# Moving two token halves against each other in a planned kernel: new distances at the stage boundaries, new head timing, new priorities

## The chip, the cores and the metric

The kernel runs on one core of a Trainium2 chip. A core has TensorE (PE, matrix products), VectorE (DVE), ScalarE (ACT), GpSimd (POOL) and SyncE (SP, which issues the DMAs); each works through its own list of instructions in order and waits at semaphores for the others. The metric is the device time of one launch in microseconds (us). Before the change it is 2561.59 us, the median of three runs (2561.55 to 2563.88).

## The reference

One step of an encoder with two layers and 1024 features, over 512 prompt tokens and 32 sample tokens. Each layer is a gated feed-forward part (FFN) of half weight, a token mixer, and a second FFN; before and after each part stands an RMS norm, and shift, scale and gate of it ("modulation") come from a conditioning vector through a matrix of 9 x 1024 columns per layer. The mixer of layer 0 is retention with 8 heads, that of layer 1 differential attention with 8 heads against keys and values made once after layer 0.

```python
for l in range(DEPTH):
    mod = (jax.nn.silu(c) @ w_ada[l] + b_ada[l]).reshape(b, N_MOD, D_MODEL)
    h = modulate(x, g_norm[l, 0], mod[:, 0], mod[:, 1])
    x = x + HALF * mod[:, 2, None] * rms_norm(swiglu(h, w_ffn_in[l, 0], w_ffn_out[l, 0]), g_norm[l, 1])
    h = modulate(x, g_norm[l, 2], mod[:, 3], mod[:, 4])
    # y: retention (l = 0) or differential attention (l = 1)
    x = x + mod[:, 5, None] * rms_norm(y, g_norm[l, 3])
    h = modulate(x, g_norm[l, 4], mod[:, 6], mod[:, 7])
    x = x + HALF * mod[:, 8, None] * rms_norm(swiglu(h, w_ffn_in[l, 1], w_ffn_out[l, 1]), g_norm[l, 5])
    if l == N_A - 1:
        k, v = shared_kv(x, c, pos, w_ada_kv, b_ada_kv, g_kv, w_kv)
```

## The kernel before

The features lie on the partitions and the 544 tokens on the free axis, cut into half A (tokens 0 to 255) and half B (the other 256 prompt tokens and the 32 sample tokens, 288 columns). Every product with a weight is cut into **units**: one block of 128 output features for one half. A unit is 6 or 8 k-steps of three matmuls (the operands are split into a high and a low part), all on line 599, 128x256 for A and 128x288 for B. There are 368 units for each half, in the order of the stages: FFN (1) of layer 0, retention, FFN (2) of layer 0, the shared keys and values, FFN (1) of layer 1, the eight query units (Q), the eight units of the attention's output product (OB), FFN (2) of layer 1.

A weight block is loaded by DMA, cast on ACT to its high part (line 578) and subtracted on DVE for its low part (line 581). Four such blocks (`w`) are held at once. If A and B use a block within a short stretch of the order, one load serves both; otherwise it is loaded and converted twice.

Between two stages each half goes through a **chain**: the last output product is added up (L918), squares are taken and summed on DVE (L824, L828), PE sums over the partitions (L711), POOL takes the root (L717), PE spreads the result (L722), DVE scales and adds into the residual stream X (L877, L880); then the same norm again for the next stage (L828, L711, L717, L722), and DVE and ACT make its eight operands (L749, L758, L764). The units of the next stage wait for these. While half A is in its chain, units of half B keep PE busy, and the other way round. `_path()` writes down, as pairs of unit numbers (a, b), how far A may be when B is at a given place. For a boundary e with entry (x, hold, y, z) of the table `BND`, A reaches e while B is x units short of it, B then goes on by `hold` units alone, and A goes y units past e before B enters; z sets over how many units the two come together before and after. The list `ATT` gives the pairs for layer 1 one by one. `plan()` turns the pairs into one list of (unit, half), interleaved evenly between two pairs.

The instruction lists of the engines are written by a list scheduler inside the kernel (`Sched`): each piece of work has a priority (smaller first), units have 1000 and their place in the list, work in the chains about 1 to 2. It takes five PSUM banks for units and three for all else; a unit's bank is free when its product has been read out, which for an FFN's output product is the addition on L918. The modulation is made in ten blocks of four PE steps (8 matmuls of 128x512 each, L504), each of which needs two loads of 1 MB; a step has the priority `ADA_HI` once its block is due, and a block comes due when the order reaches a unit number shifted by `ADA_LEAD`. `CONV_P` is the priority of the casts on ACT, `ROPE_LEAD` says how many units ahead the rotary tables are fetched, `RETH` how many retention heads may hold memory at once.

Of the kernel before, what the change touches and what calls it, by code (L numbers as in the profile page):

```python
# [49 lines left out]
def _path():  # L50
# [3 lines left out]
    for e in ((0, 1), (0, 2), "kv", (1, 0)):  # L54
        x, hold, y, z = BND.get(e, BND0)
        p += [((e, -z), (e, -z - L0)), ((e, 0), (e, -x)), ((e, 0), (e, -x + hold)), ((e, y), (e, 0)),
              ((e, y + z), (e, y + z - L0))]
    return p + [((e0, a), (e1, b)) for e0, a, e1, b in ATT]


BND0 = (7, 7, 7, 14)
BND = {(0, 1): (7, 7, 6, 10), (0, 2): (7, 7, 6, 5), 'kv': (8, 8, 6, 8), (1, 0): (0, 1, 4, 6)}
Q, OB, F2 = (1, 1), "ob", (1, 2)
ATT = [(Q, -67, Q, -75), (Q, 4, Q, -34), (Q, 8, Q, -23), (OB, 0, Q, -31), (OB, -8, Q, -13), (F2, 1, Q, -16),
       (F2, -6, Q, 0), (F2, 6, Q, -2), (F2, 37, OB, -1), (F2, 55, OB, 1), (F2, 55, F2, 0), (F2, 70, F2, -4)]
NSLOT = (34, 34)
NW = 4
NRAW = 3
# [52 lines left out]
class Sched:  # L121
# [14 lines left out]
    def go(self, gen, prio):  # L136
        self.live += 1
        self._at(self.now, [gen, prio, None], None)
# [184 lines left out]
def yoco_step(ctx: ExitStack, tc: tile.TileContext, I, O):  # L323
# [39 lines left out]
    def fa(r, n=None, o=0, p0=0, p1=P):  # L363
        n = r[1] - o if n is None else n
        return FA[p0:p1, r[0] + o:r[0] + o + n]
# [15 lines left out]
    def pe(cost, fn, pr=None):  # L381
        return ("PE", cost, fn) if pr is None else ("PE", cost, fn, pr)
# [109 lines left out]
    def ada():  # L492
        yield ready["sc"]
        yield from ada_first()
        for u in range(1, 10):
            b = yield from bank(miscb, -1)
            for k0 in range(0, 8, ADA_K):
# [3 lines left out]
                def mm(u=u, k0=k0, b=b):  # L501
                    for k in range(k0, k0 + ADA_K):
                        for g in range(4):
                            te.matmul(PS[b][32 * g:32 * g + 32, :], lhsT=SC[:, k, :],  # L504
                                      rhs=fa(ada_buf[u, k], 512, g * 512), start=(k == 0), stop=(k == 7))
                yield pe(TILED + ADA_K * 900, mm, ADA_HI if u <= due[0] else ADA_LO)
                for k in range(k0, k0 + ADA_K):
# [48 lines left out]
    def w_dma():  # L556
        for d in loads:
            u = d.unit
            r = (yield ("get", rawbuf, 1))[0]
            d.raw = (r[0], u.nk * P)  # L560

            def one(d=d, u=u, r=r):
                yield dma(u.nk * P * P * 4, fa(d.raw).rearrange("p (k f) -> p k f", f=P), u.wap, W_P.get(u.idx, 10))
                d.rawbuf = r
                S.set(d.raw_ev)
            go(one(), 0)

    def w_conv():
        for d in loads:
            w = (yield ("get", wpool, 1))[0]  # L570
            d.w = w
            yield d.raw_ev
            nk = d.unit.nk
            n = nk * P
            hi = WT[w][:, 0, :nk, :].rearrange("p k f -> p (k f)")
            lo = WT[w][:, 1, :nk, :].rearrange("p k f -> p (k f)")
            src = fa(d.raw)
            yield act(n, lambda: nc.scalar.copy(hi, src))  # L578

# [36 lines left out]
    def gate_at(n):  # L616
        ev = Ev()
        gates.append((n, ev))
        return ev
# [356 lines left out]
    def ret_prep(gate):  # L976
        yield gate
        r = yield from get(2 * NTOK, 1)
        ret["rope"] = r
        yield dma(P * 2 * NTOK * 4, fa(r), I["rope_a"], 15)  # L980
        S.set(ret["rope_ev"])
# [58 lines left out]
    def retention(hops, yevs):  # L1040
        w = I["w_in_a"][0]
        ret["rope_ev"] = Ev()
        ret["sem"] = Pool(range(RETH))
        go(ret_prep(gate_at(len(units) - ROPE_LEAD)), 15)
        st = Stage(hops)
# [276 lines left out]
    def kv_prep(gate):  # L1322
        yield gate
        r = yield from get(2 * NTOK, 1)
        kv["rope"] = r
        yield dma(P * 2 * NTOK * 4, fa(r), I["rope_b"], 15)
        S.set(kv["rope_ev"])
# [25 lines left out]
    def shared_kv(hops):  # L1353
        w = I["w_kv"]
        go(kv_prep(gate_at(len(units) - ROPE_LEAD)), 15)
        st = Stage(hops)
# [429 lines left out]
    for l in range(2):  # L1786
        m0 = 11 * l
        for s in range(3):
            if l or s:
                mark((l, s))  # L1790

            ada_due.append((max(0, len(units) + ADA_LEAD), 6 if l == 0 and s == 2 else (m0 + 3 * s + 4) // 2))
            if s != 1:
# [22 lines left out]
    go(w_dma(), 10)  # L1816
    go(w_conv(), CONV_P)
    plan()
# [7 lines left out]

TILED = 190
ADA_K = 2
ROPE_LEAD = 30
ADA_X = 4  # L1830
CT_P = -0.5
XB_P = 1.5
# [1 line left out]

TANH = (1,)
FIN_P = 0
CONV_P = 0
NEXT_P = 25
ADA_HI = 900
ADA_LO = 5000  # L1840
ADA_FIRST = 0
ADA_LEAD = -52
ARENA_N = 20600

YW = 2
RETH = 4
ATH = 3
BSEM = 3

# [112 lines left out]
```

## Time and profile before

| | |
|---|---|
| Median of three runs | 2561.59 us |
| Time of the profiled execution | 2562.68 us |
| Its span, first to last instruction | 2560.9 us |
| Mean granted TensorE clock | 0.993 |
| PE busy | 2496.2 us (97%) |
| DVE busy | 1400.1 us (55%) |
| ACT busy | 1091.3 us (43%) |
| Weight conversions on DVE (L581) | 552 |

The page names the time in which an engine worked; PE's span less its busy time is 64.7 us. The chain of work that ended last lies to 86% on PE. A share over the whole span says little here: DVE is busy for 10.87 of 50 us in one stretch and 49.58 of 50 in another, so what an idle gap of PE is worth has to be read where it stands.

### The profile page before, as it was taken

How to read it: one execution, taken by the hardware profiler on the slowest of the kernel's cores; microseconds unless marked ns; L12 is line 12 of the kernel's file. 1: busy time of each engine (PE TensorE's matmuls, PEld its weight loads, DVE VectorE, ACT ScalarE, POOL GpSimd, SP SyncE). 2: the span in 40 equal slices, each digit the busy share in tenths (PEclk: the TensorE clock that was granted, in tenths of full speed). 3: DMA queues.
4: the chain of work that ended last, by engine and by line, in shares of the span. 5: the costliest groups of instructions: out<-in, count | busy, mean ns of one | idle time of the engine just before them, and what ended most of it. 6: DMA issues, size and time to landing. Idle time of an engine off the chain costs nothing.

```text
span 2560.9 us, 48166 instructions
## 1 busy us (share of the span) xinstructions
PE 2496.2 (97%) x19848; PEld 2379.2 (93%) x19848; DVE 1400.1 (55%) x2604; ACT 1091.3 (43%) x2159; POOL 58.5 (2%) x88
## 2 busy tenths in 40 slices
PE   7999999999999999999999999999899999999998
PEld 5889999899999997999998899999699988898998
DVE  5223334955424457323338944555786987768555
ACT  4222224643333355322126533444565655465434
POOL 0000000000000000000000000000000000000000
PEclk9999999999999999999999999999899999999999
DMA  8662323642222237522226853555655445545553
GB/s 321 263 239 84 98 90 107 227 152 95 80 80 91 76 109 279 189 88 95 91 76 221 271 173 127 167 180 190 241 194 175 159 160 185 178 161 169 165 165 109
DMA packets 122235, 404.61 MB, mean 158 GB/s; under 512 B 15008, under 2 KB 33568, under 8 KB 111776
## 3 DMA queue, kind: packets, MB, share of 16 engines
q1 hardware_dynamic: 122016, 401.54, 45.9%
q8 instruction: 155, 2.54, 0.4%
q14 instruction: 64, 0.52, 0.1%
HBM read 388.25 MB, written 13.24 MB: 157 GB/s over the span
## 4 chain that ended last, share of the span: by engine, by line
PE 86%; DVE 8%; ACT 3%; issue 2%; DMA 1%; POOL 0%; SPq 0%; POOLq 0%; DVEq 0%; ACTq 0%
PE ps L599 77%; DVE w L581 2%; PE ps L504 2%; ACT w L578 1%; DVE FA L1025 1%; DVE FA L749 1%; DVE r L764 1%; PE ps L1601 1%; PE ps L1231 1%; PE ps L1219 1%; ACT FA L858 0%; PE ps L1540 0%; DMA X<-in_xb 0%; PE ps L1594 0%; DVE FA L828 0%
## 5 line engine op out<-in xcount | busy, mean ns | idle before, releaser
L599 PE MATMUL ps<-r,w 128*128 128x256 f32 (+1 forms) x17280 | 2269.4, 291 | 15.8 <-ACT r L758 11.5
L599 PEld LDWEIGHTS ps<-r,w 128*128 128x128 f32 x17280 | 2205.5, 191 | 55.7 <-issue 25.9
L581 DVE TENSOR_TENSOR w<-FA,w 128x1024 fp32r<-128x1024 f32 (+1 forms) x552 | 658.9, 1194 | 572.4 <-ACT w L578 567.5
L578 ACT CAST w<-FA 128x1024 fp32r<-128x1024 f32 (+1 forms) x552 | 564.6, 1023 | 883.5 <-PE ps L599 799.8
L965 DVE TENSOR_TENSOR FA<-ps,FA 128x256 f32<-128x256 f32 (+1 forms) x88 | 38.8, 441 | 192.5 <-PE ps L599 191.9
L929 ACT CAST r<-FA 128x288 fp32r<-128x288 f32 (+1 forms) x176 | 73.1, 416 | 107.3 <-DVE FA L965 88.3
L918 DVE TENSOR_TENSOR FA<-ps,FA 128x288 f32<-128x288 f32 (+1 forms) x144 | 62.3, 438 | 97.7 <-PE ps L599 96.2
L930 DVE TENSOR_TENSOR r<-FA,r 128x288 fp32r<-128x288 f32 (+1 forms) x176 | 76.6, 437 | 21.9 <-ACT r L929 21.5
L758 ACT ACTIVATE r<-FA,MOD 128x256 fp32r<-128x256 f32 (+1 forms) x168 | 63.1, 437 | 51.7 <-DVE FA L749 51.3
L828 DVE TENSOR_TENSOR FA<-FA 128x256 f32<-128x256 f32 (+1 forms) x168 | 73.1, 436 | 12.7 <-ACT FA L824 11.1
L504 PE MATMUL ps<-FA,SC 128*32 128x512 f32 x576 | 70.7, 605 | 5.6 <-DMA FA<-in_ada 5.6
L962 DVE SCALAR_TENSOR_TENSOR FA<-ps,FA 128x288 f32<-128x288 f32 (+1 forms) x88 | 38.4, 439 | 49.9 <-PE ps L599 49.8
L953 ACT ACTIVATE FA<-ps 128x256 f32<-128x256 f32 (+1 forms) x88 | 34.5, 393 | 69.7 <-PE ps L599 69.6
L749 DVE SCALAR_TENSOR_TENSOR FA<-X,DRV,ps 128x256 f32<-128x256 f32 (+1 forms) x168 | 57.3, 396 | 9.5 <-PE ps L722 9.3
L717 POOL TENSOR_TENSOR FA<-FA,NHALF 128x2 f32<-128x2 f32 (+1 forms) x24 | 21.7, 906 | 1774.8 <-DVE FA L715 1687.0
L858 ACT ACTIVATE FA<-FA,DRV 128x256 f32<-128x256 f32 (+1 forms) x144 | 59.1, 442 | 2.9
L764 DVE SCALAR_TENSOR_TENSOR r<-FA,MOD,r 128x256 fp32r<-128x256 f32 (+1 forms) x168 | 58.5, 400 | 0.4 <-ACT r L758 0.2
L1025 DVE TENSOR_TENSOR FA<-ps,FA 64x288 f32<-64x288 f32 (+1 forms) x128 | 56.1, 438 | 2.0
L916 ACT COPY FA<-ps 128x288 f32<-128x288 f32 (+1 forms) x96 | 36.3, 380 | 44.6 <-PE ps L599 44.6
L1021 DVE TENSOR_TENSOR FA<-ps,FA 128x256 f32<-128x256 f32 (+1 forms) x64 | 27.8, 437 | 48.9 <-PE ps L599 48.8
L504 PEld LDWEIGHTS ps<-FA,SC 128*32 128x32 f32 x576 | 14.8, 109 | 33.6 <-issue 22.4
L824 ACT ACTIVATE FA<-FA 128x256 f32<-128x256 f32 (+1 forms) x84 | 35.7, 425 | 15.5 <-DVE FA L918 14.9
(149 smaller groups left out, 1120.6 us busy)
## 6 DMA issues: line engine op xcount, KB each, us to landing
FA<-in_w_ffn_in SPq DMA_DIRECT2D x261, 512.0 KB, 3.3
FA<-in_ada SPq DMA_DIRECT2D x80, 1024.0 KB, 7.1
FA<-in_w_ffn_out SPq DMA_DIRECT2D x95, 512.0 KB, 3.5
FA<-in_w_in_a SPq DMA_DIRECT2D x58, 512.0 KB, 3.2
FA<-in_w_ffn_out SPq DMA_DIRECT2D x62, 384.0 KB, 3.1
FA<-in_w_kv SPq DMA_DIRECT2D x24, 512.0 KB, 4.4
FA<-in_w_out_a SPq DMA_DIRECT2D x20, 512.0 KB, 3.6
FA<-in_w_q_b SPq DMA_DIRECT2D x16, 512.0 KB, 3.4
```

The source lines that it names most:

```text
L504: te.matmul(PS[b][32 * g:32 * g + 32, :], lhsT=SC[:, k, :], rhs=fa(ada_buf[u, k], 512, g * 512), start=(k == 0), stop=(k == 7))
L578: yield act(n, lambda: nc.scalar.copy(hi, src))
L581: yield dve(n, lambda: nc.vector.tensor_tensor(lo, src, hi.bitcast(F32), ALU.subtract))
L599: te.matmul(PS[b][:, :n], lhsT=w[:, a, k, :], rhs=x, start=(k == 0 and j == 0), stop=(k == u.nk - 1 and j == 2))
L749: nc.vector.scalar_tensor_tensor(fa(z, c1 - c0, o), X[:, f, c0:c1], DRV[:, gi, f, s:s + 1], PS[Rb][:, o:o + c1 - c0], ALU.mult, ALU.mult)
L758: nc.scalar.activation(op.hi(H, c0, c1), fa(z, c1 - c0, o), AF.Identity, bias=MOD[:, mi, f, s:s + 1])
L764: nc.vector.scalar_tensor_tensor(op.lo(H, c0, c1), fa(z, c1 - c0, o), MOD[:, mi, f, s:s + 1], op.hi(H, c0, c1).bitcast(F32), ALU.add, ALU. ...
L828: yield dve(n, lambda: nc.vector.tensor_tensor(acc, acc, fa(t), ALU.add))
L918: yield dvp(n, lambda: nc.vector.tensor_tensor(Y[:, f, c], PS[b][:, :n], Y[:, f, c], ALU.add), 15)
L929: yield act(n, lambda: nc.scalar.copy(op.hi(H), src), pr)
L930: yield dve(n, lambda: nc.vector.tensor_tensor(op.lo(H), src, op.hi(H).bitcast(F32), ALU.subtract), pr)
L1025: nc.vector.tensor_tensor(fa(t1, n, n, x, x + 64), PS[b][y:y + 64, :n], fa(rr, n, NTOK + c.start, y, y + 64), ALU.mult)
```

## The change

Only tables and constants change; what is computed, the units and the matmuls stay as they are.

- `BND`: A goes further past three of the boundaries before B enters (y from 6 to 7, 6 to 10 and 6 to 10), and B goes on by one unit more during A's chain at two of them (hold 9 with x 8).
- `ATT`: when A reaches the queries, B is 40 units short of them and not some 36; in both versions it is 23 short when A's eight query units are through, so that now two units of B stand beside each of A's. Before the last FFN of B, A is at unit 59 of that FFN and not at 55, and three of B's output units stand before that point and not one.
- `ADA_HI` from 900 to 1100: within the first hundred places of the order the modulation's steps come behind the units, and not ahead of them. `ADA_LEAD` brings the due points six units forward.
- `CONV_P` from 0 to 1.05, `ROPE_LEAD` from 30 to 26, `RETH` from 4 to 9.

```diff
--- before.py
+++ after.py
@@ -59,10 +59,10 @@
 BND0 = (7, 7, 7, 14)
-BND = {(0, 1): (7, 7, 6, 10), (0, 2): (7, 7, 6, 5), 'kv': (8, 8, 6, 8), (1, 0): (0, 1, 4, 6)}
+BND = {(0, 1): (7, 7, 7, 12), (0, 2): (8, 9, 10, 7), 'kv': (8, 9, 10, 8), (1, 0): (7, 0, 4, 0)}
 Q, OB, F2 = (1, 1), "ob", (1, 2)
-ATT = [(Q, -67, Q, -75), (Q, 4, Q, -34), (Q, 8, Q, -23), (OB, 0, Q, -31), (OB, -8, Q, -13), (F2, 1, Q, -16),
-       (F2, -6, Q, 0), (F2, 6, Q, -2), (F2, 37, OB, -1), (F2, 55, OB, 1), (F2, 55, F2, 0), (F2, 70, F2, -4)]
+ATT = [(Q, -65, Q, -71), (Q, 0, Q, -40), (Q, 8, Q, -23), (OB, -7, Q, -35), (OB, -2, Q, -12), (F2, 1, Q, -30),
+       (F2, -12, Q, 0), (F2, 6, Q, 0), (F2, 32, OB, -2), (F2, 59, OB, 3), (F2, 51, F2, 0), (F2, 71, F2, -1)]
@@ -1826,7 +1826,7 @@
-ROPE_LEAD = 30
+ROPE_LEAD = 26
@@ -1834,16 +1834,16 @@
-CONV_P = 0
+CONV_P = 1.05
-ADA_HI = 900
+ADA_HI = 1100
-ADA_LEAD = -52
+ADA_LEAD = -58
-RETH = 4
+RETH = 9
```

The number of weight loads goes from 552 to 569, and so does the number of conversions on L581. The order of the instructions shows what the tables do. First PE before the change, where half A enters the query units: the spread of A's first norm (L722), two k-steps of B, a modulation step, and at once the sum and the spread of A's second norm and the first query unit.

```order
L722 MATMUL ps_152<-CT,FA 128x128 x2
L599 MATMUL ps_150<-r_22_129,w_144 128x288
L599 MATMUL ps_150<-r_23_130,w_144 128x288
L599 MATMUL ps_150<-r_22_129,w_144 128x288
L599 MATMUL ps_150<-r_10_117,w_144 128x288
L599 MATMUL ps_150<-r_11_118,w_144 128x288
L599 MATMUL ps_150<-r_10_117,w_144 128x288
L504 MATMUL ps_151<-FA,SC 32x512 x8
L711 MATMUL ps_153<-ONE,FA 32x2 x8
L722 MATMUL ps_153<-CT,FA 128x128 x2
L599 MATMUL ps_146<-r_20_93,w_141 128x256
```

The same place after the change; ahead of these rows, since the first norm's L722, stand 81 more matmuls of B, and behind them 12 more before the second norm's L722.

```order
L599 MATMUL ps_148<-r_22_129,w_144 128x288
L599 MATMUL ps_148<-r_23_130,w_144 128x288
L599 MATMUL ps_148<-r_22_129,w_144 128x288
L599 MATMUL ps_148<-r_10_117,w_144 128x288
L599 MATMUL ps_148<-r_11_118,w_144 128x288
L599 MATMUL ps_148<-r_10_117,w_144 128x288
L504 MATMUL ps_153<-FA,SC 32x512 x8
L711 MATMUL ps_152<-ONE,FA 32x2 x8
L599 MATMUL ps_150<-r_2_109,w_144 128x288
L599 MATMUL ps_150<-r_3_110,w_144 128x288
L599 MATMUL ps_150<-r_2_109,w_144 128x288
```

Between the two norms PE has 6 matmuls of B before the change and 87 after it, with one modulation step in both.

The second place is PE where B enters FFN (2) of layer 0, before the change: B's first unit stands right behind the spread of its norm.

```order
L599 MATMUL ps_147<-r_6_79,w_144 128x256
L599 MATMUL ps_147<-r_7_80,w_144 128x256
L599 MATMUL ps_147<-r_6_79,w_144 128x256
L722 MATMUL ps_153<-CT,FA 128x96 x3
L599 MATMUL ps_150<-r_20_127,w_142 128x288
L599 MATMUL ps_150<-r_21_128,w_142 128x288
L599 MATMUL ps_150<-r_20_127,w_142 128x288
```

The same place after the change:

```order
L722 MATMUL ps_151<-CT,FA 128x96 x3
L599 MATMUL ps_147<-r_2_75,w_142 128x256
L599 MATMUL ps_147<-r_3_76,w_142 128x256
L599 MATMUL ps_147<-r_2_75,w_142 128x256
L599 MATMUL ps_147<-r_4_77,w_142 128x256
L599 MATMUL ps_147<-r_5_78,w_142 128x256
L599 MATMUL ps_147<-r_4_77,w_142 128x256
L599 MATMUL ps_147<-r_6_79,w_142 128x256
L599 MATMUL ps_147<-r_7_80,w_142 128x256
L599 MATMUL ps_147<-r_6_79,w_142 128x256
```

Here 21 matmuls of A stand between the spread and B's first; only 9 of them are shown.

The third place is DVE where B enters the last FFN, before the change: the second of A's additions out of PSUM (L918, it frees the bank `ps_149`) stands in the middle of the work on B's operands (L749, L764).

```order
L749 SCALAR_TENSOR_TENSOR FA<-X,DRV,ps_153 128x256
L749 SCALAR_TENSOR_TENSOR FA<-X,DRV,ps_153 128x32
L918 TENSOR_TENSOR FA<-ps_149,FA 128x256
L764 SCALAR_TENSOR_TENSOR r_7_114<-FA,MOD,r_6_113 128x256
L764 SCALAR_TENSOR_TENSOR r_7_114<-FA,MOD,r_6_113 128x32
L764 SCALAR_TENSOR_TENSOR r_17_124<-FA,MOD,r_16_123 128x256
L764 SCALAR_TENSOR_TENSOR r_17_124<-FA,MOD,r_16_123 128x32
L828 TENSOR_TENSOR FA<-FA 128x256
L918 TENSOR_TENSOR FA<-ps_148,FA 128x256
```

After the change six of these additions stand ahead of that work, the first four of them even ahead of B's second norm (L715):

```order
L828 TENSOR_TENSOR FA<-FA 128x288
L918 TENSOR_TENSOR FA<-ps_148,FA 128x256
L828 TENSOR_TENSOR FA<-FA 128x288
L918 TENSOR_TENSOR FA<-ps_147,FA 128x256
L828 TENSOR_TENSOR FA<-FA 128x288
L918 TENSOR_TENSOR FA<-ps_150,FA 128x256
L828 TENSOR_TENSOR FA<-FA 128x256
L918 TENSOR_TENSOR FA<-ps_146,FA 128x256
L828 TENSOR_TENSOR FA<-FA 128x256
L715 TENSOR_SCALAR FA<-ps_151 96x3
```

PE has 30 k-steps of A (90 matmuls) between B's two norms there after the change, 36 before it.

## Rows read from the trace of the kernel before

**Rows 1.** The page, part 1: busy time, share and instructions of each engine.

```profile
PE 2496.2 (97%) x19848; PEld 2379.2 (93%) x19848; DVE 1400.1 (55%) x2604; ACT 1091.3 (43%) x2159; POOL 58.5 (2%) x88
```

**Rows 2.** PE's waits: who for whom, us in total, times, longest.

```profile
PE ps L711 <- DVE FA L828: 15.0, 6, 11.2
PE ps L599 <- ACT r L758: 11.5, 5, 5.3
```

**Rows 3.** PE by time, A enters the queries: start, length, work, [idle before].

```profile
1805.12 0.38 PE L722 MATMUL ps<-CT,FA 128*128 128x128 f32 x2
...
1808.77 1.07 PE L504 MATMUL ps<-FA,SC 128*32 128x512 f32 x8 [2.47 <-DMA FA<-in_ada]
1812.51 1.94 PE L504 MATMUL ps<-FA,SC 128*32 128x512 f32 x8 [2.67 <-DMA FA<-in_ada]
1814.71 0.39 PE L711 MATMUL ps<-ONE,FA 128*32 128x2 f32 x16 [0.27 <-DVE FA L828]
1816.21 0.69 PE L722 MATMUL ps<-CT,FA 128*128 128x128 f32 x2 [1.11 <-POOL FA L717]
...
1840.73 0.30 PE L1594 MATMUL ps<-CT,FA 128*128 128x128 f32 x1 [1.54 <-DVE FA L1585]
```

**Rows 4.** Stretches: length, busy (count) of PE, PEld, DVE, ACT, POOL, PEclk, DMA.

```profile
1818.00:1821.00 3.00, 2.93 (x12) 2.63 (x13) 3.00 (x9) 1.95 (x5) 0.00 (x0) 0.50 0.22 90
2331.00:2334.00 3.00, 3.00 (x16) 3.00 (x16) 2.38 (x8) 0.86 (x2) 0.00 (x0) 0.50 0.03 11
995.00:996.00 1.00, 1.00 (x6) 1.00 (x6) 1.00 (x5) 1.00 (x4) 0.00 (x0) 0.50 0.98 385
```

**Rows 5.** PE by time, B enters FFN (2) of layer 0.

```profile
991.37 0.41 PE L722 MATMUL ps<-CT,FA 96*128 96x96 f32 x3
993.44 0.40 PE L599 MATMUL ps<-r,w 128*128 128x288 f32 x1 [1.66 <-ACT r L758]
994.37 4.49 PE L599 MATMUL ps<-r,w 128*128 128x288 f32 x20 [0.53 <-DVE r L764]
...
1021.81 1.07 PE L504 MATMUL ps<-FA,SC 128*32 128x512 f32 x8 [0.43 <-DMA FA<-in_ada]
```

**Rows 6.** PE by time, B enters keys and values.

```profile
1420.24 0.46 PE L722 MATMUL ps<-CT,FA 96*128 96x96 f32 x3 [0.79 <-POOL FA L717]
...
1423.34 4.25 PE L599 MATMUL ps<-r,w 128*128 128x288 f32 x26 [0.66 <-DVE r L764]
...
1456.97 0.44 PE L1335 MATMUL ps<-CT,FA 128*128 128x128 f32 x2 [1.22 <-DVE FA L749]
```

**Rows 7.** PE by time, B enters the last FFN.

```profile
2300.84 0.41 PE L722 MATMUL ps<-CT,FA 96*128 96x96 f32 x3
...
2330.42 9.84 PE L599 MATMUL ps<-r,w 128*128 128x256 f32 x58 [5.35 <-ACT r L758]
```

**Rows 8.** DVE by time, the same place.

```profile
2313.57 0.45 DVE L828 TENSOR_TENSOR FA<-FA 128x288 f32<-128x288 f32 x1
...
2315.86 0.42 DVE L918 TENSOR_TENSOR FA<-ps,FA 128x256 f32<-128x256 f32 x1 [0.53 <-PE ps L599]
...
2329.86 0.41 DVE L918 TENSOR_TENSOR FA<-ps,FA 128x256 f32<-128x256 f32 x1
```

**Rows 9.** PE by time, A and then B around A's entry into the last FFN.

```profile
1993.48 0.43 PE L722 MATMUL ps<-CT,FA 128*128 128x128 f32 x2 [0.94 <-POOL FA L717]
...
2034.49 0.36 PE L711 MATMUL ps<-ONE,FA 128*32 128x2 f32 x18
```

**Rows 10.** Stretches of 50 us, columns as in rows 4.

```profile
50.00:100.00 50.00, 50.00 (x399) 42.09 (x398) 16.05 (x30) 14.37 (x24) 0.00 (x0) 1.00 0.66 246
300.00:350.00 50.00, 50.00 (x399) 50.00 (x398) 17.23 (x25) 9.85 (x11) 0.00 (x0) 1.00 0.26 85
2400.00:2450.00 50.00, 50.00 (x380) 50.00 (x379) 25.35 (x31) 21.04 (x32) 0.00 (x0) 1.00 0.49 163
```

**Rows 11.** The page, part 5: the conversions of the weights.

```profile
L581 DVE TENSOR_TENSOR w<-FA,w 128x1024 fp32r<-128x1024 f32 (+1 forms) x552 | 658.9, 1194 | 572.4 <-ACT w L578 567.5
```

## The prediction

> **What bounds the kernel.** The page's first part comes first: PE is busy for 2496.2 of 2560.9 us, DVE for 1400.1 [rows 1]. The change moves no matmul in or out, so it can only close PE's 64.7 us of idle time, or let PE run less at its lower clock. What a matmul takes does not depend on the mix: where the halves alternate, 50 us hold 399 records (125 ns each), where B is alone 380 (131.6 ns) [rows 10]; A alone is then at 2 x 125 - 131.6, about 0.12 us. A k-step of three is thus 0.36 us (A) or 0.395 us (B). A modulation step stands in the stream for 1.9 us wherever it is put.
>
> Second, PE's waits: 15.0 us for the squares' sum, of which 11.2 is the start of the launch and stays; 11.5 us for operands of the next stage [rows 2]. Third, PE by time shows where they stand: in a handful of holes, each where a half changes stage.
>
> **Hole 1, A enters the queries.** Between the first norm's spread at 1805.12 and the first query unit at 1818.02 PE waits 2.47 + 2.67 + 0.27 + 1.11 us, and 1.11 more for the first operand, 7.6 us [rows 3]. The first two are put down to the modulation's loads, but behind them stands the chain: the sum of squares was not ready before 1814.71, 9.6 us after the spread, and B had only six matmuls there. The granted clock falls to 0.50, so to 1.2 GHz: in 3 us 12 matmuls of A instead of 25 [rows 4]. Until the products are back at speed they lose about 3.3 us (some 2.4 us over 5 us of matmuls, and half a modulation step took 1.94 us where the one before took 1.07). Price of the hole: 10.9 us.
>
> With the change 87 matmuls of B (11.4 us) and a modulation step (1.9 us) stand between the two norms, 13.3 us. The chain's DVE work there was 8.7 us (8 instructions of 0.61, 7 of 0.33, one conversion and one read-out, start to start) and is now 12.5 us, for three more conversions and two more read-outs; with 0.6 us to begin and end it the cover just suffices. Between sum and spread stand 15 matmuls of B (2.0 us) for 1.5 us. Behind the spread stand 9 (1.2 us) for the 1.8 us that the first operand took [rows 3], so about 0.6 us stay, and 0.5 us in which DVE hands over operands more slowly than PE uses them. Gain 9.8 us. The first attention block's 1.54 us [rows 3] go too, mostly: two thirds of a unit more stands before that transpose. Gain 1.4 us.
>
> **Hole 2, B enters FFN (2) of layer 0.** 1.66 + 0.53 us behind the spread [rows 5], about 1 us lost while the clock is at 0.50 (6 matmuls of B in a us instead of 7.6) [rows 4], and 0.43 us for a modulation load a little later [rows 5]. The first operand came 2.07 us after the spread; 21 matmuls of A (2.5 us) cover that now, and 48 of B stand before A's entry. The modulation blocks 5 and 6 leave this place. Gain 3.3 of 3.6 us.
>
> **Hole 3, B enters keys and values.** 0.79 + 0.66 us [rows 6]: the change gives 8 k-steps for 5 between sum and spread (2.9 for 1.8 us) and 7 for 4 behind it, so both go. The 1.22 us of the value transposes [rows 6] wait for a bank that the norm holds; their place moves, and I take half. Gain 2.0 us.
>
> **Hole 4, B enters the last FFN.** 5.35 us before 2330.42 [rows 7], put down to ACT. The instruction that waits is of A (256 columns), whose operands are long there. DVE by time tells more: the addition that frees the second of A's output banks begins at 2329.86, 14 us after the first at 2315.86, because B's operands and six conversions were put ahead of it [rows 8]. With five banks PE runs dry after five units; it starts again 0.15 us after that addition ends. The clock then is 0.50 for some 6 us, 16 matmuls in 3 us [rows 4], 1.8 us. Price 7.2 us.
>
> The change puts six additions ahead of B's operands, so this hole cannot stand there. But it takes cover from the chain: between B's norms 30 k-steps of A, not 36. DVE's way from the spread at 2300.84 [rows 7] to the end of the last sum at 2314.02 [rows 8] was 13.2 us. Now the first addition, which frees the bank for the sixth output unit, stands behind eight instructions of the chain at 0.67 us, five at 0.37 and five conversions of 0.87 (start to start, as they follow each other there): 11.6 us, with the start and its own length 12.3. PE gets there after 26 k-steps, 9.5 us at the pace of these rows: a new wait of 2.8 us. Then B's first three units run at the pace of their operands, 13.5 us of DVE beside 12.7 us of PE, with 0.5 us to begin: 1.3 us. A wait of that length can bring the clock down, 1.2 us. So 5.3 us are left and 1.9 us gained.
>
> **What the change costs.** A enters the last FFN with 27 k-steps of B for 29 between the norms, and 4 for 5 between sum and spread, where 0.94 us were idle already [rows 9]: 0.8 + 0.4 = 1.2 us; bounds 0.4 and 2.5. B's chain beside A's first units of that FFN has one conversion more (1.14 us at DVE's pace) where its last sum came 0.37 us before PE's L711 at 2034.49 [rows 9]: 0.8 us; bounds 0 and 1.2.
>
> The modulation's blocks 5 and 6 now stand among retention's first heads, eight steps some 9 to 11 us apart, with 16 MB that the stretch did not move. In the old place one such step waited 0.43 us [rows 5]; at the same spacing early on, with a DMA share of 0.66 [rows 10], none did. Bounds 0 and 2.5 us (a wait of 0.3 at each), I take 1.0. Blocks 1 to 3 move from 50 to 175 us to 300 to 440 us at the old spacing, into a stretch with a DMA share of 0.26 where the old one had 0.66 [rows 10]: nothing.
>
> Seventeen more conversions are 17 x 1.194 = 20.3 us of DVE [rows 11] and as many casts on ACT. Where one half runs alone a unit needs one conversion per 2.9 us, and DVE has 1.2 us of work for it: hidden, apart from those counted in the chains above. `CONV_P` lets only a chain's first square, first operand and the norm's own steps pass a cast, 0.4 us each; three blocks lie ready ahead, 8.6 us of PE, and before's PE waits name no weight: nothing, at most 0.4 us in each of 22 norms, 9 us, were the cover gone. `RETH` and `ROPE_LEAD`: the order from the fourth retention head on is the same, and no row has PE waiting for a rotary table: nothing.
>
> **Sum.** Gains 9.8 + 1.4 + 3.3 + 2.0 + 1.9 = 18.4; costs 1.2 + 0.8 + 1.0 = 3.0; net 15.4. The profiled execution took 2562.68 us (its span and 1.8 around it), so 2547.3; it was 1.1 us above the median of the runs, which gives 2546 us.
>
> **A rule to weigh.** Rows first: from 50 to 100 us PEld is busy for 42.09 us, from 300 to 350 for 50.00, and PE has 399 records in both [rows 10]. The Trainium skill, Perfetto Trace Analysis, section Identifying the Most-Contended Engine, says that a TensorE's distance to its best is to be judged by the busy share of LDWEIGHTS and not by that of matmuls. By that rule the early stretch, from which the change takes the modulation's steps, has 7.9 us of slack in these 50 us, so some 20 over the 125 us of its steps, and the stretch to which they go has none. Equal counts in equal time speak against it in this trace; it has its place among the rivals.
>
> **Rivals.**
> *The holes move more than they close.* DVE is the engine that is late at the boundaries. Hole 4 keeps its whole price (0 instead of 1.9), hole 3 gives 1.4 and the attention block nothing, and the three costs stand at their upper bounds, 6.2: 9.8 + 3.3 + 1.4 - 6.2 = 8.3, less 1 for B's softmax whose place moves too: 2562.7 - 7.3 - 1.1 = 2554. For it: the cover in holes 1 and 4 is within 1 us of DVE's work or short of it. Against: the two largest gains do not rest on that.
> *No change that shows.* Hole 1 only moves: the query units' four blocks and banks are taken by waiting units of A, B's interleaved units cannot start, and half the gain is lost on top: 2554 + 5 = 2559. Against: six units of B stand between A's last unit before the chain and its first query unit.
> *Slower.* The 17 conversions fall into chains. On the way each costs itself and the wait for its cast, which is 567.5 us for 552 [rows 11], so 1.2 + 1.0 = 2.2 us. All 17 are 37.4 us (2584), a dozen 26.4: 2562.7 - 1.1 - 15.4 + 26.4 = 2573. From the tenth on (20.5 us) it is slower by more than a measurement can miss. Against: most stand where one half runs alone; in the chains I counted one or two more each, and these are in the sum.
> *By the slack of the weight loads* (the rule above, as a mechanism: a modulation step costs more among alternating halves early on than later): 2546 - 20 = 2526.
>
> **How the numbers follow.** The forecast has 0.66, its own range 2539 to 2551 (hole 4's rest gone altogether, or the unknown costs at their upper ends). Moved holes 0.18, no change 0.08, slower 0.06, the rule 0.02. The range of 8 in 10 reaches into the moved holes: 2537 to 2557. A measurement of this kernel tells about 0.2% (5.1 us) from no change, so faster means below 2556.5: the forecast, most of the moved holes and the rule, 0.84; the same 0.10; slower 0.06.
>
> **What would show it.** After the change: no wait above 1 us at L504, and none before the first query unit; the granted clock at 1.00 there and where B enters FFN (2); at B's entry into the last FFN a wait of 2 to 4 us just before the sum of B's second norm, beginning in the fifth or sixth of A's output units, in place of 5.35 us behind the spread; 569 conversions. The forecast is wrong if PE's idle time does not fall to between 48 and 58 us, if waits for L581 appear, or if the modulation's loads hold PE in the first retention heads.

## The result and the profile after

The changed kernel takes 2543.22 us (median of 4 runs, 2541.31 to 2544.26), the kernel before 2561.57 in the same session: ratio 0.9927, 95% interval [0.9909, 0.9944]. The forecast was 2546, with a range of 2537 to 2557. The profiled execution took 2544.26 us with a span of 2542.5; before it was 2562.68 and 2560.9, so 18.4 us less.

The page of the changed kernel, part 1 and the conversions' group of part 5, which answer to [rows 1, 11]:

```profile
PE 2488.6 (98%) x19848; PEld 2373.8 (93%) x19848; DVE 1418.0 (56%) x2621; ACT 1106.4 (44%) x2176; POOL 59.2 (2%) x88
...
L581 DVE TENSOR_TENSOR w<-FA,w 128x1024 fp32r<-128x1024 f32 (+1 forms) x569 | 679.8, 1195 | 577.5 <-ACT w L578 575.2
```

PE's count is the same. Its idle time is 2542.5 - 2488.6 = 53.9 us for 64.7 (10.8 less), and its busy time has fallen by 7.6 us with the same instructions, which is put down to the clock (the row "clock missing" in the table below). There are 17 conversions more, as the plan said.

PE's waits in the changed kernel, in us in total, times, longest, beside [rows 2]:

```profile
PE ps L711 <- DVE FA L828: 16.1, 7, 11.4
...
PE ps L599 <- ACT r L758: 3.4, 2, 3.0
PE ps L599 <- DVE FA L918: 2.9, 1, 2.9
...
PE ps L1335 <- DVE FA L749: 2.1, 1, 2.1
...
PE ps L504 <- DMA FA<-in_ada: 1.4, 2, 1.1
PE ps L599 <- ACT FA L824: 1.2, 1, 1.2
...
PE ps L599 <- DVE w L581: 0.6, 2, 0.4
```

The wait for operands (L758) went from 11.5 to 3.4 us, and what is left of it is the start of the launch. Three names are new among what PE waits for: L918, an addition that frees an output bank, L824, a square, and L581, the conversion of a weight block (0.19 us at 1435.71 and 0.41 us at 2328.39). The wait for L749, which reads the bank of a norm, grew from 1.22 us [rows 6] to 2.1.

PE by time, A enters the queries (hole 1 of the prediction), beside [rows 3]:

```profile
1781.67 11.79 PE L599 MATMUL ps<-r,w 128*128 128x288 f32 x87
1793.39 1.92 PE L504 MATMUL ps<-FA,SC 128*32 128x512 f32 x16
1795.13 0.28 PE L711 MATMUL ps<-ONE,FA 128*32 128x2 f32 x16
...
1797.99 1.82 PE L599 MATMUL ps<-r,w 128*128 128x288 f32 x10
1800.06 5.84 PE L599 MATMUL ps<-r,w 128*128 128x256 f32 x41 [0.26 <-DVE r L764]
...
1820.51 0.30 PE L1594 MATMUL ps<-CT,FA 128*128 128x128 f32 x1 [1.72 <-DVE FA L1585]
```

87 matmuls of B and one whole modulation step (16 records without a break) stand where six matmuls and two halves of a step with 2.47 and 2.67 us of waiting stood. 7.6 us of waits have become 0.26. The first attention block waits as long as ever.

PE by time, B enters keys and values (hole 3), beside [rows 6]:

```profile
1386.53 1.06 PE L504 MATMUL ps<-FA,SC 128*32 128x512 f32 x8 [1.05 <-DMA FA<-in_ada]
...
1396.55 0.36 PE L711 MATMUL ps<-ONE,FA 128*32 128x2 f32 x18 [0.90 <-DVE FA L828]
...
1399.22 0.46 PE L722 MATMUL ps<-CT,FA 96*128 96x96 f32 x3 [0.33 <-POOL FA L717]
...
1417.07 0.46 PE L722 MATMUL ps<-CT,FA 96*128 96x96 f32 x3 [0.60 <-POOL FA L717]
...
1465.93 0.44 PE L1335 MATMUL ps<-CT,FA 128*128 128x128 f32 x2 [2.11 <-DVE FA L749]
```

This place has become worse, 5.4 us of waits for 3.5. In a second profile of the same kernel (taken with one of the experiments below) it is 4.3 us; the 1.05 us at L504 are not in it.

PE by time, B enters the last FFN (hole 4), beside [rows 7], and below it DVE there, beside [rows 8]:

```profile
2295.29 0.41 PE L722 MATMUL ps<-CT,FA 96*128 96x96 f32 x3
...
2307.98 2.39 PE L599 MATMUL ps<-r,w 128*128 128x256 f32 x12 [2.91 <-DVE FA L918]
2310.30 0.49 PE L711 MATMUL ps<-ONE,FA 128*32 128x2 f32 x18
...
2317.90 2.27 PE L599 MATMUL ps<-r,w 128*128 128x288 f32 x14 [0.93 <-DVE r L764]
```

```profile
2306.19 0.94 DVE L581 TENSOR_TENSOR w<-FA,w 128x768 fp32r<-128x768 f32 x1
2307.05 0.44 DVE L828 TENSOR_TENSOR FA<-FA 128x288 f32<-128x288 f32 x1
2307.42 0.41 DVE L918 TENSOR_TENSOR FA<-ps,FA 128x256 f32<-128x256 f32 x1
```

The wait has the predicted place (just before the sum of B's second norm) and cause: PE starts 0.15 us after the first addition ends. The trace names the addition now, where it named ACT before.

The clock, in stretches of 5 us (columns as in [rows 4]); where it had been 0.50 now stands 1.00, and in this profile only the last place and the launch's tail keep a loss:

```profile
1800.00:1805.00 5.00, 4.85 (x35) 4.53 (x36) 5.00 (x12) 3.12 (x7) 0.00 (x0) 1.00 0.91 351
...
2305.00:2310.00 5.00, 2.09 (x13) 2.05 (x12) 4.92 (x12) 3.65 (x8) 0.00 (x0) 0.86 0.65 228
2310.00:2315.00 5.00, 5.00 (x51) 4.76 (x51) 3.39 (x9) 4.06 (x9) 0.85 (x1) 0.80 0.03 10
```

### The profile page after: what moved, and what is told of

Same layout as the page of the kernel before. It is cut to its first block, busy times and chain, and to the rows that moved or that the text cites. A ratio compares the mean times of both kernels' runs of the same rounds, so it can differ in the third digit from the quotient of the medians.

```text
span 2542.5 us, 48207 instructions
## 1 busy us (share of the span) xinstructions
PE 2488.6 (98%) x19848; PEld 2373.8 (93%) x19848; DVE 1418.0 (56%) x2621; ACT 1106.4 (44%) x2176; POOL 59.2 (2%) x88
## 4 chain that ended last, share of the span: by engine, by line
PE 87%; DVE 7%; ACT 2%; issue 1%; DMA 1%; POOL 0%; SPq 0%; DVEq 0%; POOLq 0%; ACTq 0%
PE ps L599 78%; DVE w L581 2%; PE ps L504 2%; ACT w L578 1%; DVE FA L1025 1%; DVE FA L828 1%; PE ps L1601 1%; PE ps L1231 1%; PE ps L1540 1%; DMA FA<-in_ada 1%; PE ps L1219 1%; DVE FA L749 1%; DMA X<-in_xb 0%; DVE FA L877 0%; PE ps L1594 0%
## 5 line engine op out<-in xcount | busy, mean ns | idle before, releaser
L599 PE MATMUL ps<-r,w 128*128 128x288 f32 (+1 forms) x17280 | 2259.1, 291 | 10.6 <-ACT r L758 3.4
L581 DVE TENSOR_TENSOR w<-FA,w 128x1024 fp32r<-128x1024 f32 (+1 forms) x569 | 679.8, 1195 | 577.5 <-ACT w L578 575.2
L578 ACT CAST w<-FA 128x1024 fp32r<-128x1024 f32 (+1 forms) x569 | 582.5, 1024 | 903.3 <-PE ps L599 804.8
L929 ACT CAST r<-FA 128x256 fp32r<-128x256 f32 (+1 forms) x176 | 72.9, 416 | 97.1 <-DVE FA L965 81.3
L918 DVE TENSOR_TENSOR FA<-ps,FA 128x288 f32<-128x288 f32 (+1 forms) x144 | 62.4, 438 | 92.3 <-PE ps L599 90.8
L930 DVE TENSOR_TENSOR r<-FA,r 128x256 fp32r<-128x256 f32 (+1 forms) x176 | 76.4, 436 | 19.0 <-ACT r L929 18.7
L758 ACT ACTIVATE r<-FA,MOD 128x256 fp32r<-128x256 f32 (+1 forms) x168 | 63.5, 437 | 47.8 <-DVE FA L749 47.5
L828 DVE TENSOR_TENSOR FA<-FA 128x288 f32<-128x288 f32 (+1 forms) x168 | 72.7, 435 | 11.0 <-ACT FA L824 9.7
L504 PE MATMUL ps<-FA,SC 128*32 128x512 f32 x576 | 69.6, 599 | 1.4 <-DMA FA<-in_ada 1.4
L749 DVE SCALAR_TENSOR_TENSOR FA<-X,DRV,ps 128x256 f32<-128x256 f32 (+1 forms) x168 | 57.7, 396 | 9.1 <-PE ps L722 8.7
L764 DVE SCALAR_TENSOR_TENSOR r<-FA,MOD,r 128x256 fp32r<-128x256 f32 (+1 forms) x168 | 58.7, 400 | 1.5 <-ACT r L758 1.4
L504 PEld LDWEIGHTS ps<-FA,SC 128*32 128x32 f32 x576 | 14.8, 109 | 29.3 <-issue 23.5
L824 ACT ACTIVATE FA<-FA 128x256 f32<-128x256 f32 (+1 forms) x84 | 35.7, 425 | 14.1 <-DVE FA L918 13.1
```

Source lines behind the costliest of these rows:

```text
L504: te.matmul(PS[b][32 * g:32 * g + 32, :], lhsT=SC[:, k, :], rhs=fa(ada_buf[u, k], 512, g * 512), start=(k == 0), stop=(k == 7))
L599: te.matmul(PS[b][:, :n], lhsT=w[:, a, k, :], rhs=x, start=(k == 0 and j == 0), stop=(k == u.nk - 1 and j == 2))
L749: nc.vector.scalar_tensor_tensor(fa(z, c1 - c0, o), X[:, f, c0:c1], DRV[:, gi, f, s:s + 1], PS[Rb][:, o:o + c1 - c0], ALU.mult, ALU.mult)
L758: nc.scalar.activation(op.hi(H, c0, c1), fa(z, c1 - c0, o), AF.Identity, bias=MOD[:, mi, f, s:s + 1])
L828: yield dve(n, lambda: nc.vector.tensor_tensor(acc, acc, fa(t), ALU.add))
L918: yield dvp(n, lambda: nc.vector.tensor_tensor(Y[:, f, c], PS[b][:, :n], Y[:, f, c], ALU.add), 15)
```

## The experiments

The table adds the waits in PE's rows by place, and the clock that was missing (5 us times one minus the granted clock, over the stretches of 5 us under 0.95, the tail left out; it counts idle time at the low clock too). Each column is one profile. How far two profiles of one kernel differ shows in the changed kernel's second: 4.3 us at hole 3 for 5.4, and 3.4 us of clock missing for 1.7. "Priorities" are CONV_P, ADA_HI, ADA_LEAD, RETH and ROPE_LEAD.

| us | before | after | ATT alone | BND alone | priorities alone | ATT + BND | both undone |
|---|---|---|---|---|---|---|---|
| first stages and retention, 60 to 940 | 8.0 | 6.0 | 7.9 | 7.2 | 6.4 | 7.1 | 6.1 |
| hole 2, B into FFN (2) | 3.2 | 0.9 | 2.8 | 0.3 | 4.6 | 0.3 | 0.3 |
| hole 3, B into keys and values | 3.5 | 5.4 | 4.0 | 1.2 | 7.1 | 1.5 | 1.4 |
| hole 1 and first attention block | 9.4 | 2.0 | 2.0 | 9.9 | 8.7 | 2.0 | 2.2 |
| A into the last FFN | 2.3 | 2.6 | 3.9 | 1.5 | 2.4 | 2.6 | 2.6 |
| hole 4, B into the last FFN | 5.6 | 4.7 | 5.0 | 5.5 | 5.8 | 4.3 | 4.6 |
| clock missing | 11.9 | 1.7 | 5.1 | 10.3 | 17.1 | 1.7 | 1.8 |
| median of the runs | 2562 | 2543.2 | 2553.0 | 2555.5 | 2565.9 | 2540.5 | 2538.7 |

**The parts alone.** The kernel before with the new ATT:

```diff
-ATT = [(Q, -67, Q, -75), (Q, 4, Q, -34), ..., (F2, 55, OB, 1), (F2, 55, F2, 0), (F2, 70, F2, -4)]
+ATT = [(Q, -65, Q, -71), (Q, 0, Q, -40), ..., (F2, 59, OB, 3), (F2, 51, F2, 0), (F2, 71, F2, -1)]
```

> The kernel before with the new numbers of ATT alone. Theory (cover): the hole at A's entry into the queries was missing work of B between the two norms, so it closes although the modulation's blocks keep their old priorities: the waits of 2.47 and 2.67 us at L504 go, the clock there is 1.00; gain about 10.5. The entry of B into the last FFN becomes a wait of about 3 us in place of 5.35 and gains 3. A's entry into the last FFN has 23 k-steps of B between the norms instead of 29 and costs 1 to 2. B's entries into FFN (2) and keys/values stay as before. Net -12: ratio 0.995, about 2549.5. Rival (loads): the two waits are for the modulation's loads, as the trace puts them down; these loads move only with the modulation's own numbers, so about 5 us of waits at L504 stay there and the net is -6: 2555.5.

Measured: 2552.97 us, ratio 0.9965 [0.9951, 0.9979], so -9.5 us. Hole 1 is closed although the modulation's blocks have their old priorities: the waits that the trace put down to their loads are gone. That fits the theory, but does not yet part it from the loads: the step between the norms now stands behind 81 more matmuls of B, so its loads have more time too. The sum was 2.5 us too good, and PE by time shows the reason, at A's entry into the last FFN with 23 k-steps of B between the norms:

```profile
1980.01 1.05 PE L599 MATMUL ps<-r,w 128*128 128x288 f32 x6 [2.63 <-DVE FA L950]
```

and the stretch behind it is at a clock of 0.66:

```profile
1980.00:1985.00 5.00, 4.99 (x40) 4.79 (x41) 2.44 (x8) 0.80 (x2) 0.84 (x1) 0.66 0.31 84
```

In the whole change 27 k-steps stand there, and the wait is 1.16 us with the clock at 1.00.

The kernel before with the new BND:

```diff
-BND = {(0, 1): (7, 7, 6, 10), (0, 2): (7, 7, 6, 5), 'kv': (8, 8, 6, 8), (1, 0): (0, 1, 4, 6)}
+BND = {(0, 1): (7, 7, 7, 12), (0, 2): (8, 9, 10, 7), 'kv': (8, 9, 10, 8), (1, 0): (7, 0, 4, 0)}
```

> The kernel before with the new numbers of BND alone. It has all of the 17 more conversions. Theory (cover): the 1.66 + 0.53 us behind the spread at B's entry into FFN (2) go, 2.5 us gained (a modulation step stays in place there); B's entry into keys and values costs 2 (from 3.5 to about 5.4 us of waits, as after); the hole at A's entry into the queries stays. Net -1: ratio 1.000, about 2560.5. Rival (conversions fall into chains): 17 more of 1.2 us each, a third of them late: 5 to 10 us slower, 2567 to 2572.

Measured: 2555.45 us, 0.9973 [0.9963, 0.9983], -7.1 us: far better than expected, and with all 17 more conversions, so the rival on them falls. The miss is hole 3: the new distances don't make it worse, they close it (1.2 us). Hole 1 stays as it was:

```profile
1797.84 1.06 PE L504 MATMUL ps<-FA,SC 128*32 128x512 f32 x8 [2.32 <-DMA FA<-in_ada]
1801.60 1.93 PE L504 MATMUL ps<-FA,SC 128*32 128x512 f32 x8 [2.70 <-DMA FA<-in_ada]
```

The kernel before with the five new priorities:

```diff
-ROPE_LEAD = 30
+ROPE_LEAD = 26
-CONV_P = 0
+CONV_P = 1.05
-ADA_HI = 900
-ADA_LEAD = -52
+ADA_HI = 1100
+ADA_LEAD = -58
-RETH = 4
+RETH = 9
```

> The kernel before with the new numbers of CONV_P, ADA_HI, ADA_LEAD, RETH and ROPE_LEAD alone. Theory (cover): the modulation steps move, but the hole at A's entry into the queries stays at 7 to 8 us with the clock at 0.50, because the chain of the norm sets its end. In B's second norms of retention and of FFN (2) no matmul of A is left between sum and spread, 1.2 us each lost. Net 0 to +2: 2561 to 2564, ratio 1.000. Rival (loads): the waits at L504 (5.6 us in all, 5.1 of them at the queries) go, and the clock comes back there: -5 to -8, 2555.

Measured: 2565.85 us, 1.0013 [1.0004, 1.0022], +3.3 us; in the profile 0.9 us of the difference is the first wait of the launch (12.07 for 11.20), which varies from profile to profile (last section). Hole 1 stays, with 1.76 + 2.66 us at L504, and behind the modulation's step PE still waits for the last of the squares, 0.27 us before [rows 3] and here 0.99:

```profile
1821.57 0.40 PE L711 MATMUL ps<-ONE,FA 128*32 128x2 f32 x16 [0.99 <-DVE FA L828]
```

So the chain sets the end of the hole: with the loads there in time PE would still have waited for it. At B's entries into FFN (2) and into keys and values no matmul of A is left between sum and spread; PE by time at the second:

```profile
1422.38 0.34 PE L711 MATMUL ps<-ONE,FA 128*32 128x2 f32 x18
1426.55 0.46 PE L722 MATMUL ps<-CT,FA 96*128 96x96 f32 x3 [3.83 <-POOL FA L717]
```

I had priced such a gap at 1.2 us; it took 2.15 and 3.83, and the clock was low behind both (the stretches of 5 us from 1005 and 1425 us at 0.73, 0.59 and 0.71, 0.61).

**What spoils hole 3.** The changed kernel with the old 'kv' numbers:

```diff
-'kv': (8, 9, 10, 8)
+'kv': (8, 8, 6, 8)
```

> The changed kernel with the old four numbers of 'kv' in BND. Theory: it is the new distance that made B's entry into keys and values worse (waits of 5.4 us for 3.5 before, the largest 2.11 us before the transposes of the values): the waits fall to 3.5 to 4, -1.5 to -2 us, about 2541.5, ratio to the kernel before 0.992. Rival: the waits there come from where the modulation's step and its load now stand (1.05 us at L504) and from the shifted transposes, and stay at 5 us or more: 2543, ratio 0.993.

Measured: 2542.83 us, 0.9924 [0.9912, 0.9937], no different from the whole change; 5.0 us of waits stay there. The distances are not the cause. The changed kernel with all five old priorities (ATT + BND):

> The changed kernel with all five old numbers of priorities and staging: BND and ATT are the new ones. Measured so far by themselves: ATT -9.5, BND -7.1, priorities +3.3 us, together -13.3, where the whole change gives about -18.5. Theory (the priorities pay only with the new distances): this kernel is at -16.6, about 2546, and B's entry into keys and values has no wait above 0.4 us, as with BND alone; what the priorities then add is -2, in the early stages. Rival (the priorities are a loss here too, and ATT and BND help each other): below the changed kernel, at 2540 to 2542.

Measured: 2540.46 us, 0.9918 [0.9904, 0.9931]. The rival holds. -21.7 us is 5.1 more than the two parts alone; 3.2 of it are read from the table (1.4 of waits, 1.8 of clock, mostly the place at 1980 us above). The clock's part is about what two profiles of one kernel differ by, so this is not shown, and the rest is not settled. At hole 3 two whole modulation steps are back between the sums of B's two norms (the changed kernel has one there), and PE waits 0.40 us before the value transposes, where it waited 2.11:

```profile
1394.88 1.92 PE L504 MATMUL ps<-FA,SC 128*32 128x512 f32 x16
...
1405.79 1.93 PE L504 MATMUL ps<-FA,SC 128*32 128x512 f32 x16
...
1411.16 0.36 PE L711 MATMUL ps<-ONE,FA 128*32 128x2 f32 x18 [0.29 <-DVE FA L828]
```

Then one number each, in the changed kernel:

```diff
-CONV_P = 1.05
+CONV_P = 0
```

> The changed kernel with CONV_P back at 0. Theory: it is the conversions' new priority that reorders B's entry into keys and values (two halves of a modulation step move between its norms, waits of 5.4 us in all against 0.3 with the distances alone): the waits there fall below 1.5 us and the kernel is 2 to 4 us faster than the changed one, ratio to before 0.991. Rival (the lead of the modulation's steps did it): 5 us stay, ratio 0.993.

```diff
-ADA_LEAD = -58
+ADA_LEAD = -52
```

> The changed kernel with ADA_LEAD back at -52. Theory (the conversions' priority did it): the waits at B's entry into keys and values stay at 4 to 6 us, ratio 0.993. Rival (the lead did it): they fall below 1.5 us, 2 to 4 us faster than the changed kernel, ratio 0.991.

Measured: 2541.37 us, 0.9920 [0.9906, 0.9933], and 2541.31 us, 0.9919 [0.9905, 0.9933]. The hole keeps 4.2 and 3.2 us, against 5.4 and 4.3 in the two profiles of the changed kernel. Neither theory holds as it was put: either number alone spoils the place. The traces show how. With only `CONV_P` taken back, one modulation step stands between the two sums, as in the changed kernel, and the larger waits come behind it:

```profile
1415.92 0.46 PE L722 MATMUL ps<-CT,FA 96*128 96x96 f32 x3 [1.09 <-POOL FA L717]
...
1461.58 0.44 PE L1335 MATMUL ps<-CT,FA 128*128 128x128 f32 x2 [2.14 <-DVE FA L749]
```

With only `ADA_LEAD` taken back, two steps stand there, but PE waits ahead of the first norm's sum, and for ACT before the value transposes:

```profile
1394.22 0.36 PE L711 MATMUL ps<-ONE,FA 128*32 128x2 f32 x18 [0.67 <-DVE FA L828]
...
1448.01 0.44 PE L1335 MATMUL ps<-CT,FA 128*128 128x128 f32 x2 [1.04 <-ACT FA L1375]
```

So both together:

```diff
-CONV_P = 1.05
+CONV_P = 0
-ADA_LEAD = -58
+ADA_LEAD = -52
```

> The changed kernel with CONV_P back at 0 and ADA_LEAD back at -52 together; ADA_HI, RETH and ROPE_LEAD keep their new values. Each of the two alone gave 2.5 us back (2541.4 and 2541.3), all five together 3 (2540.5). Theory (either of the two spoils B's entry into keys and values, the other three numbers are worth nothing): that entry has no wait above 0.5 us, and the time is that of all five undone, 2540 to 2541, ratio 0.992. Rival (the other three are a gain in the first stages): 2538 to 2539, ratio 0.991, faster than any kernel so far.

Measured: 2538.68 us (2537.90 to 2538.86), 0.9908 [0.9892, 0.9925], the fastest kernel here. The hole is at 1.4 us. That the other three numbers are worth 1.8 us over ATT + BND agrees with the rival and with the table's first line (6.1 for 7.1), but the two intervals overlap. Is the loss by the priorities real? The changed kernel again, unchanged, beside the next kernel:

> The changed kernel once more, beside the kernel below that has its BND and ATT without its priorities. Theory (the priorities are a loss of 2 to 3 us also in the changed kernel): ratio to before 0.9927, about 2543.5, and 2.5 to 4 us behind the other kernel of this call. Rival (the 2.5 us between calls were the chip): 2541, within 1 us of the other.

Measured: 2544.15 us (2542.48 to 2545.65), 0.9927 [0.9914, 0.9939]; the next kernel 2542.59. The ratio repeats; the 2.5 to 4 us to the next kernel do not come, they are 1.6, but that kernel differs from ATT + BND by one number more. By the runs' times the loss shows against "both undone", whose slowest run (2538.86) lies 2.45 us below the fastest of the changed kernel's nine (2541.31), though these are different sessions and the two 95% intervals of the ratios overlap. Against ATT + BND (2540.27 to 2541.65) even the times overlap.

**What PE waits for in hole 4.** The kernel before, with the additions of A's last eight output units ahead of B's operands on DVE:

```diff
-                    yield dvp(n, lambda: nc.vector.tensor_tensor(Y[:, f, c], PS[b][:, :n], Y[:, f, c], ALU.add), 15)
+                    yield dvp(n, lambda: nc.vector.tensor_tensor(Y[:, f, c], PS[b][:, :n], Y[:, f, c], ALU.add), pr if H == 0 else 15)
...
-            out_stage(w_out, f0, gops, pi == 0, pi == 2, yevs)
+            out_stage(w_out, f0, gops, pi == 0, pi == 2, yevs, 0.5 if pi == 2 and l == 1 and j == 1 else 15)
```

> The kernel before with one priority set: the additions of A's eight last output units in the last FFN (L918) go ahead of B's operands on DVE, at B's entry into the last FFN. PE's order there is the same up to A's last output unit. Theory (banks): the 5.35 us wait was for the addition that frees the second output bank; it falls to under 1 us and the clock there stays up, while B's first units wait some 2 to 3 us for operands that are now later. Net -4 to -5: ratio 0.998, about 2558. Rival (operands, as the trace names them): the wait stays or only moves behind A's last unit with the same size: 0 to +1, ratio 1.000.

Measured: 2561.76 us, 0.9998 [0.9989, 1.0007], nothing gained. The two halves of the theory part here. PE by time behind the spread:

```profile
2316.64 3.59 PE L599 MATMUL ps<-r,w 128*128 128x256 f32 x28
2319.83 18.36 PE L599 MATMUL ps<-r,w 128*128 128x256 f32 x139
...
2351.36 8.85 PE L599 MATMUL ps<-r,w 128*128 128x288 f32 x49 [4.91 <-DVE FA L950]
```

and on DVE:

```profile
2350.16 0.68 DVE L877 TENSOR_TENSOR FA<-FA,ps 128x512 f32<-128x512 f32 x1
2350.76 0.45 DVE L950 SCALAR_TENSOR_TENSOR FA<-FA,ps 128x288 f32<-128x288 f32 x1
```

The 5.35 us wait is gone without a rest, and B's operands, which the trace had named, are late for nobody. But 20 us later PE waits 4.91 us for L950, an instruction of B's units that frees a bank, which stands on DVE behind the work of A's chain (L877, L880); PE starts 0.15 us after it ends, and the clock falls to 0.50 there too. The mechanism (banks that late DVE instructions hold) is shown at the first place and read from the trace at the second; its price belongs to DVE's backlog at this place, and moving one instruction forward only names another.

**Two attempts to go further.** ATT + BND with one more number:

```diff
-(OB, -2, Q, -12)
+(OB, -2, Q, -13)
```

> BND and ATT of the changed kernel with the old priorities, and one number of ATT moved (the fifth entry's offset of B from -12 to -13): 29 k-steps of B stand between A's norms at its entry into the last FFN, for 27. Theory (the wait there is missing cover, 2.63 us with 23 k-steps, 1.16 with 27): it falls to 0.4 us, and the rest stays; 2540.46 - 0.8 = 2539.7, ratio 0.9915. Rival (DVE is the limit there whatever PE does): 1.1 us stay, 2540.5.

Measured: 2542.59 us, 0.9922 [0.9909, 0.9934], no faster than ATT + BND. The wait before A's second sum went (29 k-steps, as before), but 0.98 us turned up at the spread behind it, and 1.12 us for L950 later on: a miss. And ATT + BND planned with slower DVE instructions:

```diff
-    return (64 + n) / 0.96
+    return (64 + n) / 0.96 + 75
```

> BND and ATT of the changed kernel with the old priorities, and 75 ns added to what the planner takes for each DVE instruction (a 128x1024 conversion: 1.21 us for 1.13, the trace has 1.195; a 128x288 one: 0.44 for 0.37, the trace has 0.435); nothing else is changed, so only the order moves. Theory (the small waits that are left come from a plan in which DVE is too fast): PE's waits outside the start and the tail fall by 3 to 5 us, 2536. Rival (BND and ATT were fitted to the plan as it was): between sum and spread of A's norm before retention no matmul is left, and the order elsewhere shifts; +1 to +4, 2542 to 2544.

Measured: 2551.89 us, 0.9957 [0.9944, 0.9971], 11 us worse than ATT + BND. The rival's direction is right and its size far too small: the whole order moved, with seven new waits of 1.2 us and more (2.96 us at 466 us, 2.08 at 1967) in the profile, which is of the fastest of its five runs (2547.73 to 2553.39 us).

## Why the prediction held, step by step

**The sum.** Forecast for the profiled execution was -15.4 us, measured -18.4. Idle: the terms give -10.5 (15.4 less 4.9 of clock), measured -10.8. Clock: 6.1 less 1.2 = -4.9, measured -7.6. So the error of 3 us is nearly all in the clock terms; that the idle time came out so close is luck in part, because two gains that did not come were paid for by costs that did not come either.

**Hole 1, the largest term, is right** in place, size and cause. 7.6 us of waits became 0.26. That it was cover, not the modulation's loads, is shown by ATT alone (closed with the old priorities of the steps) together with the sum behind the step, which waits for the chain before the change and with the priorities alone (0.27 and 0.99 us). The clock term was too small: 3.3 us from the rows around it, while the three stretches of 5 us from 1810 to 1825 us at 0.52, 0.50 and 0.62 miss 6.8, of which some 2.5 fall on 5.2 us of idle time. Holes 2 and 4 miss 1.7 and 3.4 us, idle time included, where 1.0 and 1.8 were put.

**The attention block's 1.4 us did not come** (1.54 before, 1.72 after). The step "two thirds of a unit more stands before that transpose" counted PE only. DVE and ACT of the changed kernel there:

```profile
1817.94 0.17 DVE L1585 RECIPROCAL FA<-FA 128x2 f32<-128x2 f32 x1 [1.09 <-ACT FA L1581]
...
1818.88 1.23 DVE L581 TENSOR_TENSOR w<-FA,w 128x1024 fp32r<-128x1024 f32 x1 [0.19 <-ACT w L578]
1820.02 0.34 DVE L1588 SCALAR_TENSOR_TENSOR FA<-FA 128x128 f32<-128x128 f32 x1
```

```profile
1815.81 1.28 ACT L1581 ACT_TABLE_LOAD   x1 [1.93 <-DVE FA L1576]
```

The softmax's path holds a table load of 1.28 us, as it did before, and now a conversion of 1.23 us in it, which takes back what the longer cover gave: PE starts 0.15 us after L1588, the instruction behind it, ends.

**Hole 2 is right** (3.2 to 0.9 us of waits, the clock back); with the old priorities it is 0.3, as forecast.

**Hole 3 is the step that failed**: 2.0 us of gain were forecast, 1.9 of loss came. "8 k-steps for 5 and 7 for 4, so both go" is true of the distances (1.2 us with BND alone). I counted only k-steps, as if the two modulation steps between B's norms stayed where they were, and put `CONV_P` at nothing. With `ADA_LEAD` at -58 one step less stands between the two sums, 1.9 us of cover, and PE waits at the second spread and before the value transposes; with `CONV_P` at 1.05 it waits ahead of the first sum (0.90 us; at 1386.53 one profile of two has 1.05 us for a load as well). With either one alone taken back 4.2 and 3.2 us stay, with both 1.4. How `CONV_P` makes the first sum late was not followed on DVE.

**Hole 4 is right, with its rest**: 2.91 us where 2.8 were forecast, in the predicted unit. DVE took 12.5 us from the spread to the end of the first addition (2295.29 to 2307.83), 12.3 were forecast. B's operands then cost 0.93 us for 1.3; the 0.41 us at 2328.39 are for a conversion (L581). The clock term of 1.2 us is chance: 1.7 us are missing behind this wait here, and none behind the same wait with the old 'kv' numbers (last section).

**The costs were too high.** 3.0 us forecast; A's entry into the last FFN costs 0.3 in waits, B's chain beside it nothing, and the modulation's steps in retention hold PE nowhere above 0.4 us at L504 (the first stages gain 2.0 instead of losing 1.0). This 4.7 us pays for most of the two misses above, 5.5 us.

**The signs.** Of the signs that the prediction gave, its main ones came: 53.9 us of idle time, 569 conversions, the wait of 2.91 us in the forecast unit. Three that spoke against it came in small: 1.05 us at L504 for at most 1, waits for L581 of 0.6 us in all, and 0.38 us for a modulation load at 464.74 us, where retention begins. The conversions are not quite free, as the sum had them.

**The rivals.** The conversions in chains: 17 more in the changed kernel and in BND alone, which is 7.1 us faster; in the changed kernel they hold PE for 0.6 us. Holes that move: true of hole 3 and of the attention block, not of hole 4 and not of the costs. For the rival of the weight loads: PEld's share is 93% before and after, and where only `ADA_HI`, which moves the early modulation steps, `RETH` and `ROPE_LEAD` differ (both undone against ATT + BND) the difference is 1.8 us. The Trainium skill, Perfetto Trace Analysis, section Identifying the Most-Contended Engine, gives the busy share of LDWEIGHTS, together with the share of the peak rate that the matmuls reach, as the measure of how close TensorE is to its best. The 20 us, an estimate of the prediction by the first of the two alone, did not come in these runs.

## What to carry to other kernels

Where two streams cover each other, count what stands between a chain's instructions, in us of PE, and compare it with the slower engine's own work there, instruction by instruction; that gave the waits left at three of four places here within 1 us. Count everything that stands there, a small third stream too: what another edit of the same change takes out of the cover is lost with it. And test edits one by one even when the whole is a gain: two of these numbers cost some 5 us by the medians, and nobody would have missed them.

## What was not expected of the hardware

What a wait of 2 to 3 us costs in clock cannot be read from its length in these traces. The 2.11 us at 1465.93 in the changed kernel are followed by a clock of 1.00; the second profile of that same kernel has, at the same place and as long a wait,

```profile
1465.05 0.44 PE L1335 MATMUL ps<-CT,FA 128*128 128x128 f32 x2 [2.13 <-DVE FA L749]
...
1465.00:1470.00 5.00, 4.95 (x28) 4.80 (x29) 2.81 (x6) 3.19 (x10) 0.00 (x0) 0.66 0.86 231
```

And hole 4's wait of 2.91 us, followed by 0.86 and 0.80 in the changed kernel, leaves it at 1.00 with the old 'kv' numbers:

```profile
2307.31 1.66 PE L599 MATMUL ps<-r,w 128*128 128x256 f32 x12 [2.92 <-DVE FA L918]
...
2305.00:2310.00 5.00, 2.69 (x36) 2.57 (x37) 4.91 (x13) 3.57 (x10) 0.00 (x0) 1.00 0.62 209
2310.00:2315.00 5.00, 4.74 (x41) 4.54 (x39) 4.25 (x11) 4.90 (x11) 0.85 (x1) 1.00 0.20 50
```

So 1.7 us of clock more or less between two single profiles says nothing either. Waits of 4.9 to 5.6 us were followed by a loss each time, 3.4 us of clock missing (in the kernel before, with BND alone, with the priorities alone, and with the additions ahead); the wait of 11.20 us at the start of the launch was not, the stretches of 5 us there are at 1.00. That first wait, on the same instructions, took between 10.95 and 12.29 us in these profiles, so a difference of 1 us between two single profiles may be this wait alone.
